# Sample tokens' B rows transposed in threes and masked by VectorE alone; tail steps and weight splits placed later in the first feed-forward steps

## The chip, the cores and the metric

The kernel runs on one core of one Trainium2 chip. The metric is device time in microseconds (us) of one execution. Before the change three runs took 1756.88, 1762.55 and 1763.55 us, a median of 1762.55. The engines are called as the profile calls them: PE (TensorE matmul), PEld (its weight loads), DVE (VectorE), ACT (ScalarE), POOL (GpSimd) and SP (SyncE, which issues the DMAs).

## The reference, cut to what matters

One layer of a hybrid decoder over 1024 prompt tokens and 64 sample tokens (8 sequences of 8), width 1024, all in float32.

```python
h = rmsnorm(x, g_mix_pre) * (1 + scale_m) + shift_m
sc_b, sc_c, sc_x, z, xbc, dt_raw = jnp.split(h @ w_in, idx, axis=-1)
u = sc_c * sc_x
y_sc = sc_b * causal_dwconv(u, sc_buf, sc_conv_w)
xs, Bm, Cm = jnp.split(silu(causal_dwconv(xbc, ssm_buf, ssm_conv_w, ssm_conv_b)), ...)
# SSD, per chunk: y = (C B^T * decay) x dt + C state decay ; state = state * decay + B^T (x dt decay_to_end)
y_ssd, new_state = ssd_scan(xs, dt, A, Bm, Cm, d_skip, ssm_state)
y_ssd = rmsnorm_by_group(y_ssd * silu(z)) * ssm_norm_g
x = x + gate_m * rmsnorm(concat(y_sc, y_ssd) @ w_out, g_mix_post)
h2 = rmsnorm(x, g_ffn_pre) * (1 + scale_f) + shift_f
x = x + gate_f * rmsnorm((silu(h2 @ w_gate) * (h2 @ w_up)) @ w_down, g_ffn_post)
```

Each of the 8 sample sequences has a state of its own in every head, so its new state needs the B rows of that sequence's 8 tokens alone: B masked by sequence.

## The kernel before, in words

Every product is made of float32 parts that are split in two: a value v is rounded to `hi` (by ACT) and `lo = v - hi` (by DVE), and a product is the sum of hi·hi, hi·lo and lo·hi, so three matmuls. The helpers are `split_w` (L308 to L310) and `part` (L1023 to L1025): one ACT cast, one DVE subtraction. A weight tile must be loaded and split before PE can use it.

The stages, in order of time: input norm and first projections (to about 60 us); the SSD scan in four head groups, g = 0 to 3, with the projections of the next group laid between its steps (to about 460 us); gates and the short-convolution group (to about 800 us); output projection (to about 985 us); feed-forward, 11 steps of 256 hidden columns (to about 1470 us), its down projection and the last norm.

An order is set in two ways. Outside helper functions, the program is recorded as Python runs, and a scheduler then places the instructions of each engine; `tc.issue_after(x)` ties what follows behind x. The generators of two pieces of work are advanced in turn (`merge`, `between`), so that PE has one's matmuls while the other waits. Each engine, and SP's queue of DMAs, then runs its own list strictly in that order: an instruction that waits holds all behind it.

**The end of an SSD group.** `ssd` (from L688) runs four pairs of chunks. `part_b` (L737) multiplies chunk results and carries the state S: DVE scales S by the decay (L760) and adds the new part (L763); PE's L754 needs S. In the last of the four pairs, `sample_a` (L773) and `sample_b` (L811) were recorded ahead of `part_b`. `sample_a` transposes x and B of the 64 sample tokens, copies (ACT L799) and subtracts (DVE L800) the two parts of B into `XB`, and copies the last decay of each sequence to `dsm` (DVE L805). `sample_b` builds `BS`, the masked B rows, in six instructions of 32 partitions x 512 (L820): four on POOL, two on DVE. The sample states' products (L876) need `BS`.

**The first feed-forward steps.** The token rows are finished in two tails, `mix_tail` (L1321): `tail_a` for token tiles 4 and 5, `tail_b` for 6, 7 and the samples (8). A tail has five steps: (1) first half of the columns transposed by PE, squared by ACT, scaled by DVE; (2) second half, then the norm and the residual sum; (3) the second norm's factor and an ACT scaling of the rows (L1337); (4) and (5) transposes back (L1345) and ACT's scale and shift (L1347), with the samples' own part (L1353 to L1357, DVE and POOL) in (5). Steps are hung behind PE's blocks of `plain_step` (L1486). One `plain_step(j, q, ...)` makes the 256 hidden columns j for token half q: a gate unit and an up unit, each of four blocks of 24 matmuls, and then `inner_out` (L1503), which makes four pieces of the result and stores each: ACT cast, DVE subtraction, DMA to DRAM (`put`, L1508). All pieces of half 0 go through one buffer, `st0`, so each ACT cast of a piece waits until the DMA of the piece before has read that buffer. `plain_w` loads and splits the weights of a unit; the scheduler was free to place these splits.

Around the change this order holds: step (0,0) with gate and up, step (1,0), then half 1's first step (0,1).

Of the kernel before, what the change touches and what calls it, by code (L numbers as in the profile page):

```python
# [16 lines left out]
P = 128  # L17
# [3 lines left out]
NS = 64  # L21
# [12 lines left out]
def hymba_step(ctx, tc, i, o):  # L34
# [42 lines left out]
    def st(shape, dt=F32):  # L77
        return stp.tile(shape, dt, tag="st", name=nm("st"))
# [10 lines left out]
    def const(shape, name, dt=F32):  # L89
        return cp.tile(shape, dt, tag=name, name=name)  # L90

    def bc(ap, axis, n):
        shape = list(ap.shape)
        shape.insert(axis, n)
        return ap.unsqueeze(axis).broadcast_to(shape)
# [58 lines left out]
    for k in range(4, KT):  # L154
# [18 lines left out]
                            pattern=[[-8, 8]], channel_multiplier=1)  # L173
    nc.gpsimd.affine_select(out=blk, in_=blk, compare_op=ALU.is_ge, fill=0.0, base=7,
                            pattern=[[8, 8]], channel_multiplier=-1)
    blk4 = const([NS, 4], "blk4")
    nc.vector.tensor_tensor(blk4, blk[:, 0:4], blk[:, 4:8], op=add)
    i2 = const([32, 16], "i2")
    nc.vector.tensor_tensor(i2, ident[:32, 0:16], ident[:32, 16:32], op=add)
    selc = const([64, 16], "selc")  # L180
# [382 lines left out]
    r = 0  # L563
# [123 lines left out]
    def ssd(g, x0, x1, Bf, Cf):  # L687
# [86 lines left out]
        def sample_a():  # L774
            tpx, tpb = pz(), pz()
            for p in range(2):
                nc.tensor.transpose(tpx[:NS, p * P:(p + 1) * P], xc[p][:, col:], ident)
            nc.tensor.transpose(tpb[:NS, 0:P], Bf[:, col:], ident)
            mm(tpb[:NS, P:P + NS], Bf[:, col:], Cf[:, col:], start=True, stop=True)
            ac = pz()  # L780
            for r in range(4):
                mm(ac[:, r * NS:(r + 1) * NS], sel(4 * g + r), acT[:, col:], start=True, stop=True)
            xd = st([NS, 2, 4, 64])
            for e, factor in enumerate((dt, edend)):
                nc.vector.tensor_tensor(xd[:, e], tpx[:NS, :256].rearrange("p (r q) -> p r q", r=4),
                                        bc(factor[:NS, 8, hs], 2, 64), op=mult)
            EC = st([P, 3, 4, NS])
            acv = ac[:, :256].rearrange("p (r l) -> p r l", r=4)
            E, Cx = EC[:NS, 0], EC[:, 1]
            nc.scalar.activation(Cx, acv, AF.Exp)  # L790
            nc.vector.tensor_tensor(E, acv[:NS], bc(acum[:NS, 8, hs], 2, NS), op=sub)
            nc.vector.tensor_scalar(E, E, 0.0, None, op0=mn)
            nc.scalar.activation(E, E, AF.Exp)
            CBm = EC[:NS, 2, 0, :]
            nc.vector.tensor_tensor(CBm, tpb[:NS, P:P + NS], utsf, op=mult)

            XB = gzp.tile([96, 768], F32R, tag="gz", name=nm("XB"))
            Bp = XB[:NS, 512:768].rearrange("k (j n) -> k j n", j=2)
            nc.scalar.copy(Bp[:, 0, :], tpb[:NS, 0:P])  # L799
            nc.vector.tensor_tensor(Bp[:, 1, :], tpb[:NS, 0:P], Bp[:, 0, :], op=sub)  # L800
            nc.vector.tensor_tensor(E, E, bc(CBm, 1, 4), op=mult)
            dsm = sp.tile([P, 2, 8], F32, tag="dsm", name=nm("dsm"))
            for p in range(2):
                for h in range(2):
                    nc.vector.tensor_copy(dsm[64 * h:64 * h + 64, p, :],  # L805
                                          bt(Cx[64 * h:64 * h + 64, 2 * p + h, :])[:, :, 7])
            nc.vector.tensor_tensor(Cx, Cx, bc(Cf[:, col:], 1, 4), op=mult)
            return xd, E, Cx, XB, Bp, dsm

        def sample_b(xd, XB, Bp):  # L810
            XS = XB[:, 0:512].rearrange("k (q m) -> k q m", q=2)  # L811
            BS = fm(F32R)[:96, :1024].rearrange("k (q n) -> k q n", q=2)
            for q in range(2):
                own, other = slice(32 * q, 32 * q + 32), slice(32 - 32 * q, 64 - 32 * q)
                v = xd[own, 1].rearrange("k r q -> k (r q)")
                nc.scalar.copy(XS[own, q, :], v)
                nc.scalar.copy(XS[64:96, q, :], v)
                nc.vector.tensor_tensor(XS[other, q, :], v, XS[own, q, :], op=sub)
                for part, at in ((0, own), (0, other), (1, slice(64, 96))):
                    (nc.vector if part else nc.gpsimd).tensor_tensor(  # L820
                        BS[at, q, :].rearrange("k (b n) -> k b n", b=4), bc(Bp[own, part, :], 1, 4),
                        bc(blk4[own], 2, P), op=mult)
            return XS, BS

        def sample_states(p):
# [14 lines left out]
        for j in range(4):  # L840
            if j < 3:
                a2 = part_a(j + 1)
            else:
                a2 = sample_a()
                XS, BS = sample_b(a2[0], *a2[3:5])
            yield
            part_b(j, *a, *m)
            yield
            if j < 3:
                a = a2  # L850
                m = part_m(j + 1, *a)
                yield
# [559 lines left out]
    def plain_x(xp, q):  # L1412
# [10 lines left out]
        X_of[q][3] = new_x(xp, 3, q, b22)  # L1423
        yield

    def behind(gen):

        while True:
            queued = {x.engine: x for x in nc.cur_bb.bb.instructions}
            with ExitStack() as es:  # L1430
                for e in (nc.vector, nc.scalar):
                    es.enter_context(tc.issue_after(queued[e.engine]))
                if next(gen, gen) is gen:
                    return
            yield

    def sums_x(xp, q):
# [17 lines left out]
    def plain_unit(W, q, put, between={}):  # L1455

        X = X_of[q]

        def block(ps, i, h):
            acc3(ps, QS[q][1], [(W[i, j][0][k], W[i, j][1][k], x[0][k], x[1][k])  # L1460
                                for j, x in enumerate((X[(1, 0)[h]], X[(2, 3)[h]])) for k in range(4)])

        for n, (i, h) in enumerate(((0, 0), (0, 1), (1, 0), (1, 1))):
            ps = (pm, pz)[q]()
            in_order(block, ps, i, h)
            put(i, h, ps[:, :QS[q][1]])
            for gen in between.get(n, ()):
                in_order(next, gen, None)
# [9 lines left out]
    def gate_unit(j, qs, W, between={}):  # L1478
# [3 lines left out]
        for q in qs:  # L1482
            v = G_[j, q].rearrange("p m h c -> p (m h c)")
            nc.scalar.activation(v, v, AF.Silu)

    def plain_step(j, q, between):  # L1486

        sg, f = blocks(in_turn(sg_from[q]), q, "sg"), blocks(in_turn(f_from[q]), q, "f")
        plain_unit(plain_w(w_gate, 256 * j), q, lambda i, h, ps: nc.scalar.activation(sg[:, i, h], ps, AF.Silu),
                   between[0])  # L1490
        plain_unit(plain_w(w_up, 256 * j), q,
                   lambda i, h, ps: nc.vector.tensor_tensor(f[:, i, h], sg[:, i, h], ps, op=mult), between[1])
        inner_out(j, q, f, nc.vector)

# [53 lines left out]
    run(px)  # L1548
    out_proj(2, terms[2], {7: [tail_a]}, lambda mp: w_last, (3,))
    tail_b = mix_tail([6, 7, 8], x_tl, row_tl, G2)  # L1550
    plain_step(0, 0, ({0: [tail_b], 1: [tail_b], 2: [tail_a, tail_a], 3: [tail_a]}, {3: [tail_b, tail_b]}))
    raw_from = [btp] * 4
    w_from = [slots[1]] * 4 + [slots[0]] * 4
    g0 = sums_x([xc0], 0)
    s0 = behind(g0)
    plain_step(1, 0, ({0: [tail_b]}, {1: [s0], 2: [s0], 3: [s0]}))
    run(tail_a, tail_b)
    tailp.close()
    xc1 = [pool(left, "xc1a", 1)]
# [177 lines left out]
```

## Time and profile before

| what | value |
|---|---|
| median of 3 runs | 1762.55 us |
| the profiled execution | 1764.2 us, its span 1762.5 us |
| PE busy | 1693.1 us, 96% of the span |
| PE weight loads | 1605.9 us |
| DVE, ACT, POOL busy | 1173.0, 773.5, 231.8 us |
| mean granted TensorE clock | 0.985 |
| HBM traffic | 146 GB/s over the span |

PE is busy nearly everywhere, so what can be won or lost is PE's idle time and the time in which its clock is granted at half. A busy PE is the union of its matmuls' modelled spans, so the share hardly says how fast they run; the clock column of a stage does. A wait row reads: engine, tile and line that waited, what it waited for, total us, times, longest.

### The profile page before, as it was taken

The page shows a single profiled execution, that of the slowest core. Times are in us where ns is not written, and L with a number is a line of the kernel's source. Part 1 is how long each engine was busy: PE and PEld are TensorE (multiplying, and loading weights), DVE is VectorE, ACT ScalarE, POOL GpSimd, SP SyncE. Part 2 cuts the span into 40 slices and gives each one's busy share as a digit, 9 for nine tenths or more (in the row PEclk, how much of TensorE's full clock was granted, in tenths as well). Part 3 has the DMA queues.
Part 4 walks back from the last instruction along what each step waited for, and adds up shares of the span by engine and source line. Part 5 has one row for each costly group of instructions (what it writes and reads, how often), then busy time and mean ns, then how long its engine had stood idle before and what let it go on. Part 6 is the DMA issues. An engine that isn't in the chain of part 4 may idle for free. (4 is left out here: it accounts for less than half of the span.)

```text
span 1762.5 us, 31586 instructions
## 1 busy us (share of the span) xinstructions
PE 1693.1 (96%) x12624; PEld 1605.9 (91%) x12624; DVE 1173.0 (67%) x2263; ACT 773.5 (44%) x1595; POOL 231.8 (13%) x333
## 2 busy tenths in 40 slices
PE   5999999999999999999999899999999999899997
PEld 4898888899999999998989899999999998799987
DVE  5578787867797676651137769666665575678845
ACT  3447454557344333322227765444444454322303
POOL 2111020201000000000000000122222201322303
PEclk9999999999899999999999999999999999999999
DMA  9301345442312422268275634344444439755243
GB/s 314 74 19 43 104 130 182 129 126 76 125 49 99 150 78 66 86 215 283 71 243 188 201 114 149 105 149 147 148 151 143 147 134 347 288 223 229 100 153 120
DMA packets 160634, 259.74 MB, mean 147 GB/s; under 512 B 10561, under 2 KB 124401, under 8 KB 158182
## 3 DMA queue, kind: packets, MB, share of 16 engines
q1 hardware_dynamic: 160486, 257.71, 42.8%
q8 instruction: 99, 1.62, 0.4%
q14 instruction: 49, 0.40, 0.1%
HBM read 186.30 MB, written 71.38 MB: 146 GB/s over the span
## 5 line engine op out<-in xcount | busy, mean ns | idle before, releaser
L310 DVE TENSOR_TENSOR wl<-raw,wh 128x512 fp32r<-128x512 f32 (+1 forms) x87 | 61.4, 730 | 101.2 <-ACT wh L309 97.5
L333 PE MATMUL pm<-h,wh 128*128 128x384 f32 (+1 forms) x342 | 115.2, 337 | 0.0
L332 PE MATMUL pm<-h,wh 128*128 128x384 f32 (+1 forms) x342 | 115.1, 337 | 0.0
L334 PE MATMUL pm<-h,wl 128*128 128x384 f32 (+1 forms) x342 | 114.4, 336 | 0.0
L334 PE MATMUL pm<-hb,wl 128*128 128x512 f32 (+2 forms) x320 | 107.4, 337 | 1.9 <-DVE wl L310 1.9
L333 PE MATMUL pm<-hb,wh 128*128 128x512 f32 (+2 forms) x320 | 107.3, 337 | 0.0
L332 PE MATMUL pm<-hb,wh 128*128 128x512 f32 (+2 forms) x320 | 105.4, 337 | 1.3 <-ACT wh L309 1.3
L309 ACT CAST wh<-raw 128x512 fp32r<-128x512 f32 (+1 forms) x89 | 56.5, 664 | 109.8 <-PE pm L333 66.7
L1025 DVE TENSOR_TENSOR fs<-f,fs 128x512 fp32r<-128x512 f32 (+1 forms) x80 | 55.4, 706 | 25.9 <-ACT fs L1024 25.4
L1024 ACT CAST fs<-f 128x512 fp32r<-128x512 f32 (+1 forms) x80 | 46.7, 598 | 49.9 <-DMA f_d<-fs 31.6
L334 PEld LDWEIGHTS pm<-hb,wl 128*128 128x128 f32 x320 | 60.7, 190 | 7.4 <-DVE wl L310 2.1
L332 PEld LDWEIGHTS pm<-h,wh 128*128 128x128 f32 x342 | 65.5, 192 | 1.9 <-issue 1.0
L1080 DVE TENSOR_TENSOR facc<-facc,pz 128x288 f32<-128x288 f32 x124 | 55.9, 451 | 16.7 <-PE pz L1065 16.4
L332 PEld LDWEIGHTS pm<-hb,wh 128*128 128x128 f32 x320 | 60.5, 190 | 7.0 <-ACT wh L309 1.6
L333 PEld LDWEIGHTS pm<-h,wh 128*128 128x128 f32 x342 | 65.4, 191 | 1.1 <-issue 0.3
L334 PEld LDWEIGHTS pm<-h,wl 128*128 128x128 f32 x342 | 65.4, 191 | 0.9 <-issue 0.9
L333 PEld LDWEIGHTS pm<-hb,wh 128*128 128x128 f32 x320 | 60.7, 190 | 5.2
L1080 DVE TENSOR_TENSOR facc<-facc,pm 128x256 f32<-128x256 f32 x124 | 51.5, 415 | 6.5 <-PE pm L1065 6.3
L332 PE MATMUL pm<-bt,wh 128*128 128x384 f32 (+1 forms) x146 | 51.4, 352 | 0.0
L1042 POOL TENSOR_TENSOR raw<-raw 128x512 f32<-128x512 f32 x16 | 22.5, 1404 | 206.7 <-DVE raw L1040 206.7
L334 PE MATMUL pm<-bt,wl 128*128 128x384 f32 (+1 forms) x146 | 48.5, 332 | 0.3 <-DVE wl L310 0.2
L333 PE MATMUL pm<-bt,wh 128*128 128x384 f32 (+1 forms) x146 | 48.1, 330 | 0.0
(7508 smaller groups left out, 6405.7 us busy)
## 6 DMA issues: line engine op xcount, KB each, us to landing
raw<-in_w_in SPq DMA_DIRECT2D x48, 512.0 KB
fc<-f_d SPq DMA_DIRECT2D x9, 2016.0 KB
f_d<-fs SPq DMA_DIRECT2D x31, 576.0 KB
wa<-in_w_ada SPq DMA_DIRECT2D x32, 512.0 KB
raw<-in_w_out SPq DMA_DIRECT2D x32, 512.0 KB
fc<-f_d SPq DMA_DIRECT2D x9, 1792.0 KB
f_d<-fs SPq DMA_DIRECT2D x31, 512.0 KB
raw<-in_w_gate SPq DMA_DIRECT2D x28, 512.0 KB
```

The source lines that it names most:

```text
L309: (nc.gpsimd.tensor_copy if hi_eng else nc.scalar.copy)(wh, raw)
L310: (eng or nc.vector).tensor_tensor(wl, raw, wh, op=sub)
L332: mm(ps[:, :n], wh, xh, start=(first and j == 0), stop=False)
L333: mm(ps[:, :n], wh, xl, start=False, stop=False)
L334: mm(ps[:, :n], wl, xh, start=False, stop=(last and j == end))
L1024: nc.scalar.copy(hi, v)
L1025: (eng or nc.vector).tensor_tensor(lo, v, hi, op=sub)
L1042: eng.tensor_tensor(a21, a11, a21, op=sub)
L1080: nc.vector.tensor_tensor(out(q, i, h), out(q, i, h), ps, op=add)
```

## The change

1. `sample_a`: ACT first copies B of the sample tokens three times side by side (into an unused part of the tile `EC`), and two transposes of 96 rows (one for each half of the tokens) set B's rows on partitions 0 to 31, 32 to 63 and 64 to 95. The CB product moves to other columns of the same bank. One ACT copy of 96 x 256 and one DVE subtraction of 32 x 256 make the parts.
2. `sample_b`: the six masking instructions become two on DVE, of 64 x 1024 and of 32 x 1024. POOL has none. The constant `blk4` grows to 96 rows.
3. `sample_b` is recorded behind `part_b` of the last pair.
4. First feed-forward steps: `tail_b`'s second step one block later; `tail_a`'s steps 3, 4, 5 at gate block 3, up blocks 0 and 1 (before: two at gate block 2, one at 3); `tail_b`'s step 4 at the next step's gate block 0, step 5 at its block 1.
5. `step_w`: in every step with j > 0 that is made by `plain_step`, that is step (1,0), the loads and splits of both weight units are recorded through `last_in_line`, which ties their first instruction on DVE and ACT behind everything recorded so far on these engines.

```diff
-    blk4 = const([NS, 4], "blk4")
-    nc.vector.tensor_tensor(blk4, blk[:, 0:4], blk[:, 4:8], op=add)
+    blk4 = const([96, 4], "blk4")
+    nc.vector.tensor_tensor(blk4[:NS], blk[:, 0:4], blk[:, 4:8], op=add)
+    nc.vector.tensor_copy(blk4[NS:], blk4[:32])
...
-            nc.tensor.transpose(tpb[:NS, 0:P], Bf[:, col:], ident)
-            mm(tpb[:NS, P:P + NS], Bf[:, col:], Cf[:, col:], start=True, stop=True)
+            EC = st([P, 3, 4, NS])
+            B3 = EC[:, 2, 1:4].rearrange("p a (h n) -> p (a h) n", h=2).rearrange("p (q r) n -> p q r n", q=2)
+            nc.scalar.copy(B3, bc(Bf[:, col:].rearrange("p (q n) -> p q n", q=2), 2, 3))
+            for q in range(2):
+                nc.tensor.transpose(tpb[:96, q * P:(q + 1) * P], B3[:, q].rearrange("p r n -> p (r n)"), ident)
+            mm(tpb[:NS, 256:256 + NS], Bf[:, col:], Cf[:, col:], start=True, stop=True)
...
-            Bp = XB[:NS, 512:768].rearrange("k (j n) -> k j n", j=2)
-            nc.scalar.copy(Bp[:, 0, :], tpb[:NS, 0:P])
-            nc.vector.tensor_tensor(Bp[:, 1, :], tpb[:NS, 0:P], Bp[:, 0, :], op=sub)
+            Bp = XB[:, 512:768]
+            nc.scalar.copy(Bp, tpb[:96, 0:256])
+            nc.vector.tensor_tensor(Bp[NS:], tpb[NS:96, 0:256], Bp[NS:], op=sub)
...
-                for part, at in ((0, own), (0, other), (1, slice(64, 96))):
-                    (nc.vector if part else nc.gpsimd).tensor_tensor(
-                        BS[at, q, :].rearrange("k (b n) -> k b n", b=4), bc(Bp[own, part, :], 1, 4),
-                        bc(blk4[own], 2, P), op=mult)
+            for at in (slice(0, NS), slice(NS, 96)):
+                nc.vector.tensor_tensor(BS[at].rearrange("k q (b n) -> k q b n", b=4),
+                                        bc(Bp[at].rearrange("k (q n) -> k q n", q=2), 2, 4),
+                                        bc(bc(blk4[at], 1, 2), 3, P), op=mult)
...
                 a2 = sample_a()
-                XS, BS = sample_b(a2[0], *a2[3:5])
             yield
             part_b(j, *a, *m)
+            if j == 3:
+                XS, BS = sample_b(a2[0], *a2[3:5])
             yield
...
+    def last_in_line(f, *a):
+
+        queued = {x.engine: x for x in nc.cur_bb.bb.instructions}
+        with ExitStack() as es:
+            for e in (nc.vector, nc.scalar):
+                es.enter_context(tc.issue_after(queued[e.engine]))
+            return f(*a)
+
     def behind(gen):
...
+        while last_in_line(next, gen, gen) is not gen:
             yield
...
+    def step_w(w, j):
+        return last_in_line(plain_w, w, 256 * j) if j else plain_w(w, 256 * j)
+
...
-        plain_unit(plain_w(w_gate, 256 * j), q, lambda i, h, ps: nc.scalar.activation(sg[:, i, h], ps, AF.Silu),
+        plain_unit(step_w(w_gate, j), q, lambda i, h, ps: nc.scalar.activation(sg[:, i, h], ps, AF.Silu),
                    between[0])
-        plain_unit(plain_w(w_up, 256 * j), q,
+        plain_unit(step_w(w_up, j), q,
                    lambda i, h, ps: nc.vector.tensor_tensor(f[:, i, h], sg[:, i, h], ps, op=mult), between[1])
...
-    plain_step(0, 0, ({0: [tail_b], 1: [tail_b], 2: [tail_a, tail_a], 3: [tail_a]}, {3: [tail_b, tail_b]}))
+    plain_step(0, 0, ({0: [tail_b], 2: [tail_b], 3: [tail_a]}, {0: [tail_a], 1: [tail_a], 3: [tail_b]}))
...
-    plain_step(1, 0, ({0: [tail_b]}, {1: [s0], 2: [s0], 3: [s0]}))
+    plain_step(1, 0, ({0: [tail_b], 1: [tail_b]}, {1: [s0], 2: [s0], 3: [s0]}))
```

Lines below the first hunk have other numbers after the change (L1024 becomes L1031, L310 becomes L312, and so on). Numbers behind a tile's name tell buffers apart; those of the two kernels don't match.

VectorE at the end of group 0, before (`wl` is the low part of the next group's first weight tile, `st`, `XB`, `dsm` and `fm` are the sample tokens' tiles, `S` the carried state):

```order
L310 TENSOR_TENSOR wl_1978<-raw_1975,wh_1977 128x1024
L791 TENSOR_TENSOR st_1811<-pz_1803,acum 64x256
L800 TENSOR_TENSOR XB_1817<-pz_1798,XB_1817 64x128
L792 TENSOR_SCALAR st_1811<-st_1811 64x256
L805 COPY dsm_1821<-st_1811 64x8 x4
L818 TENSOR_TENSOR XB_1817<-st_1808,XB_1817 32x256
L801 TENSOR_TENSOR st_1811<-st_1811 64x256
L807 TENSOR_TENSOR st_1811<-st_1811,fm_1311 128x256
L820 TENSOR_TENSOR fm_1827<-XB_1817,blk_259 32x512
L818 TENSOR_TENSOR XB_1817<-st_1808,XB_1817 32x256
L820 TENSOR_TENSOR fm_1827<-XB_1817,blk_259 32x512
L763 TENSOR_TENSOR S_1882<-S_1882,pz_1866 128x256
```

The weight split stands ahead of all the sample work, and the addition to S behind all of it.

The same engine and place after the change; L826 is the masking that was L820, L765 the addition to S, L425 to L429 a convolution of the next group, L312 the weight split:

```order
L813 TENSOR_TENSOR st_1802<-st_1802,fm_1312 128x256
L762 TENSOR_TENSOR S_1872<-S_1736,ecd 128x256
L824 TENSOR_TENSOR XB_1820<-st_1812,XB_1820 32x256
L765 TENSOR_TENSOR S_1872<-S_1872,pz_1856 128x256
L824 TENSOR_TENSOR XB_1820<-st_1812,XB_1820 32x256
L762 TENSOR_TENSOR S_1879<-S_1872,ecd 128x256
L826 TENSOR_TENSOR fm_1884<-XB_1820,blk_259 64x1024
L765 TENSOR_TENSOR S_1879<-S_1879,pz_1856 128x256
```

Both additions to S now stand ahead of the second masking instruction. Further on in the same list, the end of the convolution and what follows it:

```order
L428 SCALAR_TENSOR_TENSOR fm_1939<-ext_1771,vT,fm_1939 128x1024
L429 SCALAR_TENSOR_TENSOR fm_1939<-ext_1771,vT,fm_1939 128x64
L868 COPY st_1952<-pz_1949 128x256
L312 TENSOR_TENSOR wl_1977<-raw_1974,wh_1976 128x1024
L884 TENSOR_TENSOR s_237_1893<-s_237_1893,dsm_1824 128x1024
L884 TENSOR_TENSOR s_251_2007<-s_251_2007,dsm_1824 128x1024
```

The split of `wl_1977`, the same tile as `wl_1978` before, has moved from ahead of the sample work to behind the masks, the convolution and the copy L868. On PE the first matmuls that need it (L336) have moved behind the other parts of the next group's first blocks and the first two sample states' products.

ScalarE where step (0,0) passes into step (1,0), before (`fs` are the stored pieces of step (0,0), `wp` 1195 to 1198 the gate weights of step (1,0), `sg` a gate block's result, L1337 the rows' scaling, L1347 the samples' and tokens' scale and shift):

```order
L1337 ACTIVATE x_10152<-x_10152,sm_10469 64x1024
L1024 CAST wp__1195_10527<-raw_10523 128x512
L1024 CAST wp__1196_10530<-raw_10525 128x512
L1024 CAST wp__1197_10533<-raw_10523 128x512
L1024 CAST wp__1198_10536<-raw_10525 128x512
L1347 ACTIVATE acc_8215<-pz_10485,modT,A_f 128x256
L1347 ACTIVATE acc_8215<-pz_10489,modT,A_f 128x256
L1347 ACTIVATE acc_8215<-pz_10493,modT,A_f 128x256
L1347 ACTIVATE acc_8215<-pz_10497,modT,A_f 128x256
L1024 CAST fs_10501<-f_10105 128x512
L1489 ACTIVATE sg_10521<-pm_10539 128x256
```

The weights' casts stand ahead of every stored piece; the other three pieces are cast later still. The same after the change, where the gate weights are `wp` 1191 to 1194:

```order
L1344 ACTIVATE x_10145<-x_10145,sm_10462 64x1024
L1031 CAST fs_10478<-f_10098 128x512
L1031 CAST fs_10482<-f_10098 128x256
L1031 CAST fs_10488<-f_10098 128x512
L1031 CAST fs_10494<-f_10098 128x512
L1031 CAST wp__1191_10504<-raw_10500 128x512
L1031 CAST wp__1192_10507<-raw_10502 128x512
L1031 CAST wp__1193_10510<-raw_10500 128x512
L1031 CAST wp__1194_10513<-raw_10502 128x512
L1500 ACTIVATE sg_10498<-pm_10516 128x256
```

All four pieces now stand ahead of the first weight, and the four casts L1354 that stood between have gone behind the gate block. VectorE's subtractions of these tiles follow in the same order.

ScalarE during step (0,0)'s gate blocks, before, where the up weights of step (1,0), `wp` 1210 and 1211, were first cast (L1229 and L355 belong to the tails):

```order
L1489 ACTIVATE sg_10104<-pm_10122 128x256
L1024 CAST wp__1210_10688<-raw_10684 128x512
L355 ACTIVATE tl_9978,ssn<-x_9974 128x1024
L1024 CAST wp__1211_10691<-raw_10686 128x512
L355 ACTIVATE tl_9979,ssn<-x_9976 128x1024
L1229 ACTIVATE tl_10154,ss_10157<-pz_10159 128x512
L1229 ACTIVATE tl_10155,ss_10157<-pz_10166 128x512
L1489 ACTIVATE sg_10104<-pm_10180 128x256
```

The casts are spread between the tails' work, a whole unit ahead of their use.

ScalarE where step (1,0) passes from gate to up, after (`wp` 1210 to 1213 are its up weights, 1233 and 1234 a part of the next step's, `x__1227` the samples' operand of half 1):

```order
L1500 ACTIVATE sg_10498<-pm_10625 128x256
L1031 CAST x__1227_10841<-acc_8208 128x1152
L1031 CAST wp__1233_10853<-raw_10848 128x512
L1031 CAST wp__1234_10856<-raw_10846 128x512
L1500 ACTIVATE sg_10498<-pm_10651 128x256
L1031 CAST wp__1210_10681<-raw_10677 128x512
L1031 CAST wp__1211_10684<-raw_10679 128x512
L1031 CAST wp__1212_10687<-raw_10677 128x512
L1031 CAST wp__1213_10690<-raw_10679 128x512
```

The same up weights now stand behind the last gate block's evacuation of step (1,0), behind `x__1227` and behind two weights of the next step.

More of the change, by code (lines that the diff above doesn't have):

```diff
@@ L786, in sample_a @@
                                         bc(factor[:NS, 8, hs], 2, 64), op=mult)
-            EC = st([P, 3, 4, NS])
             acv = ac[:, :256].rearrange("p (r l) -> p r l", r=4)
@@ L794, in sample_a @@
             CBm = EC[:NS, 2, 0, :]
-            nc.vector.tensor_tensor(CBm, tpb[:NS, P:P + NS], utsf, op=mult)
+            nc.vector.tensor_tensor(CBm, tpb[:NS, 256:256 + NS], utsf, op=mult)
             XB = gzp.tile([96, 768], F32R, tag="gz", name=nm("XB"))
-            Bp = XB[:NS, 512:768].rearrange("k (j n) -> k j n", j=2)
-            nc.scalar.copy(Bp[:, 0, :], tpb[:NS, 0:P])
-            nc.vector.tensor_tensor(Bp[:, 1, :], tpb[:NS, 0:P], Bp[:, 0, :], op=sub)
+            Bp = XB[:, 512:768]
+            nc.scalar.copy(Bp, tpb[:96, 0:256])
+            nc.vector.tensor_tensor(Bp[NS:], tpb[NS:96, 0:256], Bp[NS:], op=sub)
             nc.vector.tensor_tensor(E, E, bc(CBm, 1, 4), op=mult)
@@ L1424, in plain_x @@
         yield
-    def behind(gen):
[L1428 to L1434, printed above, removed]
+    def last_in_line(f, *a):
[4 more added lines that the diff above has]
+            return f(*a)
+    def behind(gen):
+        while last_in_line(next, gen, gen) is not gen:
             yield
```

## The prediction

> **What bounds the kernel now.** I read the page first, then PE's waits, then the stretches around the two longest. In the page's row of engines each entry is the busy time, its share of the span and the instructions:
>
> ```profile
> PE 1693.1 (96%) x12624; PEld 1605.9 (91%) x12624; DVE 1173.0 (67%) x2263; ACT 773.5 (44%) x1595; POOL 231.8 (13%) x333
> ```
>
> PE sets the time. What the change can touch is PE's idle time and its half-clock time. The waits of PE in its places are (total, times, longest):
>
> ```profile
> PE pz L754 <- DVE S L763: 4.5, 2, 2.8
> PE pz L1228 <- DVE tl L1230: 3.1, 1, 3.1
> PE pz L1345 <- ACT x L1337: 3.1, 2, 2.7
> ```
>
> The first is the end of SSD groups 0 and 3; the other two stand in the first feed-forward steps. The windows show the steps, a clean comparison behind them, and the clock at the end of groups 0 and 3 (after the engines: PEclk, DMA share, GB/s):
>
> ```profile
> core 0: us, PE busy (x) PEld busy (x) DVE busy (x) ACT busy (x) POOL busy (x), PEclk, DMA share, GB/s
> ...
> 175.28:182.00 6.72, 3.94 (x19) 3.69 (x19) 6.65 (x14) 1.07 (x4) 0.74 (x2) 0.75 0.00 1
> ...
> 441.36:444.77 3.41, 1.70 (x16) 1.26 (x15) 3.38 (x8) 1.35 (x3) 0.00 (x0) 1.00 0.00 0
> 444.77:448.18 3.41, 3.41 (x16) 3.37 (x15) 2.84 (x7) 1.84 (x4) 0.00 (x0) 0.50 0.00 0
> ...
> 455.01:461.84 6.83, 6.83 (x47) 5.80 (x46) 3.19 (x9) 0.10 (x1) 0.00 (x0) 0.50 0.25 77
> ...
> 986.26:1011.61 25.35, 19.04 (x139) 17.17 (x138) 20.61 (x67) 17.41 (x42) 0.13 (x1) 0.93 0.59 202
> 1011.61:1023.36 11.75, 11.75 (x100) 11.75 (x100) 3.54 (x8) 6.70 (x11) 0.00 (x0) 1.00 0.01 1
> ```
>
> Half clock comes in pieces of 3.41 us and follows a gap: PE was busy 1.70 of 3.41, and the next 3.41 ran at 0.50. Such a piece costs PE half of itself, 1.7 us. Group 0's stretch holds one too (0.75 over 6.72 us).
>
> **The tail's transposes (part 4): a gain.** PE's rows in the first stretch:
>
> ```profile
> 989.21 1.47 PE L1228 MATMUL pz<-ident,acc 128*128 128x128 f32 x12
> ...
> 997.09 1.65 PE L1228 MATMUL pz<-ident,acc 128*128 128x128 f32 x8 [3.09 <-DVE tl L1230]
> ...
> 1005.45 0.65 PE L1345 MATMUL pz<-ident,x 128*128 128x128 f32 x4 [2.75 <-ACT x L1337]
> 1006.49 0.66 PE L1345 MATMUL pz<-ident,x 128*128 128x128 f32 x4 [0.39 <-ACT x L1337]
> ...
> 1010.06 1.79 PE L1345 MATMUL pz<-ident,x 128*128 128x128 f32 x8
> ```
>
> Four blocks take 11.75 us where nothing disturbs them. The first stretch holds four blocks and 40 transposes; at 1.47 / 12 = 0.12 us these are 4.8, so 25.35 - 16.55 = 8.8 us are lost: 6.2 of idle time, 1.7 of clock (0.93 is 1 - 0.07, and 0.07 x 25.35 = 1.8 of half clock's loss), the rest bank waits. Each awaited step now stands one block, 2.9 us, later or more, so the three waits go. What is late next is the bank: 8 transposes took 1.79 instead of 0.96, and two such groups leave 2 x 0.8 = 1.6. The gain is **7.2** (5 to 8).
>
> **Weights behind the stores (part 5, gate): a loss.** Step (1,0)'s first gate weight now stands on ACT and DVE behind all four stored pieces of step (0,0), which share one buffer. Rows of the chain:
>
> ```profile
> 1025.73 0.63 ACT L1024 CAST fs<-f 128x512 fp32r<-128x512 f32 x1
> ...
> 1037.81 0.68 DVE L1025 TENSOR_TENSOR fs<-f,fs 128x512 fp32r<-128x512 f32 x1
> 1041.26 0.62 ACT L1024 CAST fs<-f 128x512 fp32r<-128x512 f32 x1 [2.70 <-DMA f_d<-fs]
> ...
> 1058.10 0.42 DVE L1025 TENSOR_TENSOR fs<-f,fs 128x256 fp32r<-128x256 f32 x1
> 1061.14 0.62 ACT L1024 CAST fs<-f 128x512 fp32r<-128x512 f32 x1 [0.16 <-DVE f L1521]
> ```
>
> A store blocks the next cast from the end of the subtraction, 1037.81 + 0.68 = 1038.49, to 1041.26: 2.77 us. For the half-sized piece the bound is 1061.14 - 1058.52 = 2.6. In before the weights stood ahead of this, so the 2.77 hid behind PE's block. Now, from the end of PE's last up block: the product 0.42 (by its size, as the 128x256 row); piece 1, 0.63 + 0.68; store 2.77; piece 2, 0.42 + 0.42; store 2.6; piece 3, 0.63 + 0.68; store 2.77; piece 4's cast 0.62, then DVE's subtraction 0.68 and the weight's own, of the same size, 0.68. That is 14.0 us. PE has two matmuls that need the rounded part alone, and nothing else: the tail steps are hung behind the gate block. So **+13.8** idle (13 to 14.5; lower if piece 2's store is faster). PE then restarts at half clock; one piece is 1.7 (0 to 3.4). Together **+15.5**.
>
> **Weights behind the evacuation (part 5, up): a loss.** The up weights now stand behind the samples' operand `x__1227`, whose steps read:
>
> ```profile
> 1028.09 0.71 PE L1353 MATMUL pz<-ident,x 64*128 64x64 f32 x8
> 1029.14 4.31 POOL L1357 TENSOR_TENSOR acc<-acc,modT 128x64 f32<-128x64 f32 x8 [26.92 <-DVE acc L1356]
> 1033.49 1.16 ACT L1024 CAST x__1227_10848<-acc 128x1152 fp32r<-128x1152 f32 x1 [0.15 <-POOL acc L1357]
> ...
> 1035.27 1.35 DVE L1025 TENSOR_TENSOR x__1227_10848<-acc,x__1227_10848 128x1152 fp32r<-128x1152 f32 x1
> ```
>
> From PE's L1353 (28.80) to the cast's end (34.65) are 5.85 us; then 1.35 and two weight splits of 0.68 on DVE make 8.6. PE covers it with gate blocks 2 and 3 and two matmuls, 5.9 + 0.2. The wait is **+2.5** (0 to 4), and with one chance in two of a half-clock piece +0.8: **+3.3**.
>
> Behind both, DVE is full where half 1 begins, and PE waited for it there once:
>
> ```profile
> 1049.15:1080.75 31.60, 30.86 (x230) 30.45 (x229) 30.89 (x43) 18.51 (x30) 0.00 (x0) 1.00 0.31 111
> 1080.76 0.40 PE L1065 MATMUL pz<-x__1227_10848,w__1267_11175 128*128 128x288 f32 x1 [0.74 <-DVE w__1267_11175 L1025]
> ```
>
> The splits moved later join this queue, 30.89 busy of 31.60: **+1.0** (0 to 3). The tail in all: -7.2 + 15.5 + 3.3 + 1.0 = **+12.6**.
>
> **The samples' part (1 to 3): a small gain in group 3, a trade in group 0.** Group 0's rows:
>
> ```profile
> 168.79 1.21 DVE L310 TENSOR_TENSOR wl<-raw,wh 128x1024 fp32r<-128x1024 f32 x1
> 168.53 1.28 ACT L790 ACT_TABLE_LOAD   x1
> 170.24 0.42 DVE L791 TENSOR_TENSOR st<-pz,acum 64x256 f32<-64x256 f32 x1 [0.24 <-ACT st L790]
> 170.44 4.65 POOL L820 TENSOR_TENSOR fm<-XB,blk 32x512 fp32r<-32x512 f32 x4 [7.85 <-ACT XB L799]
> 171.54 2.20 DVE L805 COPY dsm<-st 64x8 f32<-64x8 f32 x4
> 178.06 0.72 PE L754 MATMUL pz<-st,S 128*64 128x128 f32 x8 [2.78 <-DVE S L763]
> 179.40 0.47 DVE L767 SCALAR_TENSOR_TENSOR fm<-fm,dcol,pz 128x256 f32<-128x256 f32 x1
> 180.51 0.81 DVE L423 TENSOR_SCALAR fm<-ext,vT 128x1024 f32<-128x1024 f32 x1
> ...
> 185.44 0.28 DVE L427 SCALAR_TENSOR_TENSOR fm<-ext,vT,fm 128x64 f32<-128x64 f32 x1
> 185.84 1.03 PE L832 MATMUL pz<-ident,s 128*128 128x128 f32 x8
> ...
> 189.27 0.62 PE L876 MATMUL pz<-fm,XB 96*128 96x512 f32 x2
> 189.82 0.64 PE L870 MATMUL pz<-st,st 128*64 128x8 f32 x16
> ```
>
> While POOL masked, a `dsm` copy took DVE 0.55 us. All sixteen such copies of the run (least, median and most in ns):
>
> ```profile
> L805 DVE COPY dsm<-st x16: 154/542/922, 171.5 to 437.2; 64x8 f32<-64x8 f32 x16
> ```
>
> I take the least, 0.15, for all of them after the change. A mask over 1024 columns should need 1.21, as the split at 168.79 does.
>
> The sample work on DVE starts at about 168.9 rather than 170.24, since ACT's table load now stands ahead of the copy that held it, and the split is gone from here. Eight instructions of at most 0.42 and four copies of 0.15 bring S to 172.8. PE comes there with 18 products of 0.15 still ahead of its old stop at 175.28, so at 172.5: a wait of 0.3, and the 2.78 goes. But the split now follows masks, convolution and a copy. On DVE: three of 0.42 and a mask to S's second addition, 175.3; two updates of 0.47 and a mask, 177.4; the convolution (180.51 to 185.72) 5.2, 182.6; the copy 0.42, 183.0; the split, **184.2**. PE meanwhile has moved forward what needs no `wl`: half of the S products 0.36, two transposes of S 0.25 (by the eight in 1.03), four sample products 0.2 and sixteen 0.64, eight transposes 1.03, six weight products 1.1 (384 columns, by 11.75 / 96 for 256), two state products 0.62. These 4.2 us put it at 175.28 + 4.2 + 0.3 = 179.8. The new wait is 4.4 and the net 4.4 + 0.3 - 2.8 = **+1.9** (-2 to +4; the low end is a wait of 2.2 with no half-clock piece, 1.7, in its wake).
>
> In group 3 no such split moves. The 1.71 and the piece of 1.7 behind it go, and of the 6.83 us at 0.50 later (3.4 lost) I take 1.0 as following from the same gap: **-4.4** (-1.7 to -6.8). Groups 1 and 2 show no wait: 0. An extra transpose a group, 4 x 0.12, is +0.5. The sum here is 1.9 - 4.4 + 0.5 = **-2.0**. The work taken from POOL hid behind PE wherever DVE did not stand still for it, and costs nothing.
>
> In all 12.6 - 2.0 = +10.6. The profiled execution has a span of 1762.5, and with what lies around it 1764.2; the median is 1762.55, which I take as the base: **1773.2 us**.
>
> **A rule on the clock.** Here 1.71 us of idle time was enough for half clock. The Trainium skill's "TensorE: Matmul & The Clock Gate", section "HAM oscillation — how this bites in real kernels", warns of idle gaps above about 3.4 us. By that rule the 0.8 of the up wait would fall away and the time would be 1772.4. This trace speaks against the threshold with its 1.71.
>
> **Rivals.** *Half clock ends throughout groups 0 and 3, so the kernel is not slower beyond what can be told:* 6.8 instead of 4.4 in group 3 and 1.7 in group 0 give 4.1 less, 1769.1. It decides from 1.8 below my sum. For it: a gap stands ahead of the piece at 444.77; against: at 455 PE was not idle, and group 0 keeps a gap by my own sum. *The trade in group 0 is dearer:* if ACT's table load still comes when it did, `wl` is 1.4 later; with a second half-clock piece behind the long stall, 1.7, and DVE's queue at 3 instead of 1, 1778.3. *The change does not do what it says:* if DVE's copies stay at 0.55 without POOL's masks, S is late as before and group 3's 4.4 is not won: 1777.6. *The stores do not serialise three times:* if only one waits, 2.77 + 2.6 less, 1767.8.
>
> **How the numbers follow.** About 0.5%, 8.8 us, is what a measurement of this kernel can tell from no change, so 1771.4 divides "slower" from "same". My forecast has 0.52 (its own range 1769 to 1777, two thirds above the line); the clock rival 0.18, the dear trade 0.15, the unchanged masks 0.05, the stores 0.06. The 0.04 left is for faster: the gate stall would have to be absent (1757.7) and the clock rival true besides (1753.6, below the other line at 1753.7). Slower: 0.34 + 0.15 + 0.05 + 0.02 = 0.56; same: 0.18 + 0.16 + 0.06 = 0.40. The range 1764 to 1780 takes in all but the ends.
>
> **What would show it.** Right: a PE gap of 13 to 14 us ahead of step (1,0)'s first gate block, released by DVE or ACT on a `wp` tile, with casts of `fs` waiting for DMAs in it, and half clock behind it; a gap of about 2.5 ahead of its up unit; no L1230 wait near 994; in group 0 a wait for `wl` instead of S; `dsm` copies near 0.15. Wrong: PE running through that boundary, or stores that end within a block.

## The result, and the profile after

The changed kernel takes 1775.3 us, the median of 6 runs (1769.9 to 1779.13), beside 1762.72 (1756.88 to 1763.55, 6 runs) before. The ratio is 1.0073, 95% interval 1.0051 to 1.0095: it is slower by 12.9 us (9 to 17). The prediction was 1773.2, 10.6 more. Its profiled execution has a span of 1775.4 us.

PE's waits after the change, in the places that the prediction speaks of and in two that it doesn't (`wp__653` and `h`):

```profile
PE pm L334 <- ACT wp__1191_10504 L1031: 12.8, 1, 12.8
...
PE pm L336 <- DVE wp__653_5031 L1032: 2.6, 1, 2.6
...
PE pz L883 <- DVE st L868: 2.1, 1, 2.1
...
PE pm L334 <- ACT wp__1210_10681 L1031: 1.8, 1, 1.8
PE pz L1352 <- ACT x L1344: 1.6, 2, 1.2
...
PE pm L1070 <- ACT h L1031: 1.2, 1, 1.2
```

The waits for S (4.5) and for `tl` (3.1) are gone. In their place stands one gap of 12.8 us, ahead of step (1,0)'s first gate block, as forecast. ACT's list in it shows the chain (start, duration, and in brackets how long ACT stood idle ahead of the cast and what ended it):

```profile
1020.75 0.62 ACT L1031 CAST fs<-f 128x512 fp32r<-128x512 f32 x1 [1.79 <-DVE f L1503]
1024.80 0.40 ACT L1031 CAST fs<-f 128x256 fp32r<-128x256 f32 x1 [3.43 <-DMA f_d<-fs]
1027.78 0.62 ACT L1031 CAST fs<-f 128x512 fp32r<-128x512 f32 x1 [2.58 <-DMA f_d<-fs]
1031.83 0.62 ACT L1031 CAST fs<-f 128x512 fp32r<-128x512 f32 x1 [3.43 <-DMA f_d<-fs]
1032.35 0.61 ACT L1031 CAST wp__1191_10504<-raw 128x512 fp32r<-128x512 f32 x1
```

Three casts wait for the DMA of the piece before, and only then comes the weight. VectorE's and PE's rows of the same chain:

```profile
1021.40 0.69 DVE L1032 TENSOR_TENSOR fs<-f,fs 128x512 fp32r<-128x512 f32 x1 [0.68 <-ACT fs L1031]
1025.23 0.43 DVE L1032 TENSOR_TENSOR fs<-f,fs 128x256 fp32r<-128x256 f32 x1 [3.14 <-ACT fs L1031]
...
1028.43 0.69 DVE L1032 TENSOR_TENSOR fs<-f,fs 128x512 fp32r<-128x512 f32 x1 [0.94 <-ACT fs L1031]
...
1033.02 0.58 PE L334 MATMUL pm<-x__1114_9935,wp__1191_10504 128*128 128x256 f32 x1 [12.76 <-ACT wp__1191_10504 L1031]
```

From the end of a subtraction to the next cast are 1024.80 - 1022.09 = 2.71, 1027.78 - 1025.66 = 2.12 and 1031.83 - 1029.12 = 2.71 us (forecast 2.77, 2.6, 2.77). The gap, the stretch of half clock behind it, and what follows (PEclk is the first number behind the engines):

```profile
core 0: us, PE busy (x) PEld busy (x) DVE busy (x) ACT busy (x) POOL busy (x), PEclk, DMA share, GB/s
1020.26:1033.02 12.76, 0.00 (x1) 0.00 (x1) 4.47 (x9) 2.83 (x6) 0.00 (x0) 0.65 0.25 103
1033.02:1037.63 4.61, 4.59 (x20) 4.30 (x21) 2.56 (x5) 1.51 (x3) 0.00 (x0) 0.50 0.55 180
1037.63:1049.73 12.10, 12.04 (x102) 11.53 (x101) 6.09 (x13) 9.72 (x17) 4.32 (x8) 1.00 0.18 63
```

PE then ran 4.6 us at half clock, which costs 2.3, and at full clock from there to the up unit's wait. In group 0 the wait is now this (rows of DVE and PE, in order of time):

```profile
182.57 0.41 DVE L868 COPY st<-pz 128x256 f32<-128x256 f32 x1
182.91 1.21 DVE L312 TENSOR_TENSOR wl<-raw,wh 128x1024 fp32r<-128x1024 f32 x1
...
183.04 0.73 PE L883 MATMUL pz<-fm,XB 96*128 96x512 f32 x2 [2.12 <-DVE st L868]
...
184.17 0.59 PE L336 MATMUL pm<-bt,wl 128*128 128x384 f32 x1 [0.40 <-DVE wl L312]
```

And the `dsm` copies, without POOL's masks beside them:

```profile
L811 DVE COPY dsm<-st x16: 153/166/170, 169.5 to 439.6; 64x8 f32<-64x8 f32 x16
```

To compare places in two traces I subtract the times of the same instruction. PE's wait ahead of group 0 that ends at 130.00 us (before at 129.15) comes 0.85 later; that is ahead of all that was changed in the work. The end of the tail's region (PE's wait for `w__1267` ended at 1095.42, before at 1080.76) comes 14.66 later, its start (the wait for `wl` ended at 948.50, before at 945.14) 3.36 later. So 11.3 us of the 12.9 lie in the first feed-forward steps, 2.5 between 130 and 945 us, and behind 1095 the changed kernel regains 1.8.

### The profile page after: what moved, and what is told of

Read it like the earlier page. It is cut to its first block, busy times and chain, and to the rows that moved or that the text cites. A ratio compares the mean times of both kernels' runs of the same rounds, so it can differ in the third digit from the quotient of the medians.

```text
span 1775.4 us, 31579 instructions
## 1 busy us (share of the span) xinstructions
PE 1694.9 (95%) x12628; PEld 1608.4 (91%) x12628; DVE 1167.5 (66%) x2264; ACT 778.1 (44%) x1601; POOL 213.8 (12%) x317
## 4 chain that ended last, share of the span: by engine, by line
PE 79%; DVE 9%; DMA 5%; ACT 3%; issue 2%; POOL 1%; SPq 1%; DVEq 0%; POOLq 0%; ACTq 0%
PE pm L334 10%; PE pm L336 10%; PE pm L335 9%; PE pz L1072 7%; PE pz L1070 7%; PE pz L1071 7%; PE pm L1070 6%; PE pm L1072 6%; PE pm L1071 6%; DMA h<-in_w_ada 1%; DMA raw<-in_w_in 1%; PE pm L209 1%; PE pz L751 1%; PE pz L745 1%; PE pz L756 1%
## 5 line engine op out<-in xcount | busy, mean ns | idle before, releaser
L312 DVE TENSOR_TENSOR wl<-raw,wh 128x512 fp32r<-128x512 f32 (+1 forms) x87 | 61.3, 729 | 100.8 <-ACT wh L311 97.4
L336 PE MATMUL pm<-h,wl 128*128 128x384 f32 (+1 forms) x342 | 115.0, 337 | 0.0
L336 PE MATMUL pm<-hb,wl 128*128 128x512 f32 (+2 forms) x320 | 107.4, 337 | 1.9 <-DVE wl L312 1.9
L1031 ACT CAST fs<-f 128x512 fp32r<-128x512 f32 (+1 forms) x80 | 46.6, 597 | 59.3 <-DMA f_d<-fs 37.5
L336 PEld LDWEIGHTS pm<-hb,wl 128*128 128x128 f32 x320 | 60.8, 190 | 7.4 <-DVE wl L312 2.1
L336 PEld LDWEIGHTS pm<-h,wl 128*128 128x128 f32 x342 | 66.1, 193 | 1.3 <-issue 1.0
L334 PE MATMUL pm<-bt,wh 128*128 128x384 f32 (+2 forms) x146 | 52.0, 356 | 0.0
L336 PE MATMUL pm<-bt,wl 128*128 128x384 f32 (+1 forms) x146 | 48.8, 334 | 0.6 <-DVE wl L312 0.6
L335 PE MATMUL pm<-bt,wh 128*128 128x384 f32 (+2 forms) x146 | 48.1, 330 | 0.0
```

The costliest lines, as they stand in the source:

```text
L312: (eng or nc.vector).tensor_tensor(wl, raw, wh, op=sub)
L334: mm(ps[:, :n], wh, xh, start=(first and j == 0), stop=False)
L335: mm(ps[:, :n], wh, xl, start=False, stop=False)
L336: mm(ps[:, :n], wl, xh, start=False, stop=(last and j == end))
L1031: nc.scalar.copy(hi, v)
```

## The experiments

Ten kernels, each timed in five rounds against the kernel before on the same chip. Differences in us are the ratio less one, times 1762. The theory is the prediction's: the weights behind the stores (part 5) make the loss, part 4 wins, and the samples' part (1 to 3) about breaks even. The rival that the first trace raised is that the samples' part loses, behind group 3, where the waits for `wp__653` and `h` are new.

**Part 5 undone.**

```diff
     def step_w(w, j):
-        return last_in_line(plain_w, w, 256 * j) if j else plain_w(w, 256 * j)
+        return plain_w(w, 256 * j)
```

> Parts 1 to 4 with part 5 undone. If the 14 us stall in front of step (1,0) and the wait at its up unit come from the weights tied behind the stores (part 5), both are gone from the profile and the kernel takes 1763 - 7.2 (tail) - 2.0 (samples) = 1753 to 1757 us. If the stall comes from the new places of the tail steps (part 4), it stays and the time stays near 1775.

Measured 1758.34 us, ratio 0.998 (0.9971 to 0.9989), -3.5 us. The gap of 12.8 and the up unit's wait are gone from the trace. So part 5 costs 1.0073 - 0.998 = 0.0093, 16 us. The time is 1 us over the upper end of what was expected: the other parts win less. Its trace also shows a new wait of 1.65 us for ACT's `sg`, near 1071 us where half 1 begins; the kernel before and the one with part 4 alone have none there.

**Parts 1 to 3 alone** (the lines of parts 4 and 5 set back).

> Parts 1 to 3 alone. By the prediction's sum 2.0 us less than before, 1760.7; by the rival that the half-clock pieces of groups 0 and 3 go, 6.1 less, 1756.6; by the dear trade in group 0, 0 to 2 us more, 1763 to 1765. The profile of the full change shows a wait of 2.6 for a weight behind group 3, which was 0.9: if the samples' part makes it, it is seen here too and the time is 1764 or more.

1763.05 us, 1.0004 (0.9994 to 1.0014). The waits behind group 3 are here too, so the samples' part makes them. PE's rows there, of this kernel: the norm's products L291, where VectorE's stretch begins, and the three waits:

```profile
461.61 1.50 PE L291 MATMUL pz<-ident,sm 128*128 128x128 f32 x12
...
483.08 0.46 PE L336 MATMUL pm<-bt,wp__653_5031 128*128 128x384 f32 x1 [2.59 <-DVE wp__653_5031 L1032]
...
522.79 0.39 PE L1070 MATMUL pm<-h,w__683_5285 128*128 128x272 f32 x1 [1.21 <-ACT h L1031]
...
523.95 0.39 PE L1071 MATMUL pm<-h,w__683_5285 128*128 128x272 f32 x1 [0.77 <-DVE h L1032]
```

The same instructions of the kernel before:

```profile
464.96 1.60 PE L289 MATMUL pz<-ident,sm 128*128 128x128 f32 x12
...
486.09 0.44 PE L334 MATMUL pm<-bt,wp__653_5038 128*128 128x384 f32 x1 [0.91 <-DVE wp__653_5038 L1025]
...
524.55 0.39 PE L1064 MATMUL pm<-h,w__683_5292 128*128 128x272 f32 x1 [0.52 <-DVE h L1025]
```

At L291 this kernel is 3.35 us ahead, at `wp__653` 3.0, at the last 0.6. It wins three microseconds in the SSD stage and gives them back in the next 60. VectorE shows why; the windows are from L291 to the first of these waits and from there to the second, before:

```profile
464.96:486.03 21.07, 20.22 (x128) 19.68 (x127) 19.72 (x29) 9.53 (x17) 0.00 (x0) 1.00 0.69 231
486.03:523.65 37.62, 37.13 (x248) 36.70 (x248) 37.27 (x60) 16.92 (x33) 0.00 (x0) 1.00 0.19 57
```

and with parts 1 to 3:

```profile
461.61:483.02 21.41, 18.88 (x121) 18.34 (x120) 20.21 (x30) 9.60 (x17) 0.00 (x0) 1.00 0.67 228
483.02:522.80 39.78, 38.52 (x248) 38.29 (x248) 37.32 (x60) 16.77 (x33) 0.00 (x0) 0.96 0.18 54
```

DVE is busy 37.3 of 37.6 us before, so it has nothing to spare there, and PE's waits in this stretch end with VectorE's work or with a cast. In the first window PE now has 18.9 us of work instead of 20.2, and waits for about the same 20 us of DVE. In the second DVE has the same 37.3 us of work, and what makes it 2.2 us longer is PE's waits and two half-clock pieces that follow them, 3.4 us lost:

```profile
483.38:486.79 3.41, 3.41 (x12) 3.41 (x11) 3.41 (x7) 1.04 (x2) 0.00 (x0) 0.50 0.07 6
524.34:527.75 3.41, 3.41 (x18) 3.41 (x17) 1.61 (x4) 0.53 (x2) 0.00 (x0) 0.50 0.00 0
```

**Part 4 alone.**

```diff
-    plain_step(0, 0, ({0: [tail_b], 1: [tail_b], 2: [tail_a, tail_a], 3: [tail_a]}, {3: [tail_b, tail_b]}))
+    plain_step(0, 0, ({0: [tail_b], 2: [tail_b], 3: [tail_a]}, {0: [tail_a], 1: [tail_a], 3: [tail_b]}))
...
-    plain_step(1, 0, ({0: [tail_b]}, {1: [s0], 2: [s0], 3: [s0]}))
+    plain_step(1, 0, ({0: [tail_b], 1: [tail_b]}, {1: [s0], 2: [s0], 3: [s0]}))
```

> Part 4 alone. Prediction: the waits at 994 and 1003 and the half-clock piece between them go, 7.2 us less than before, 1755.5 (5 to 8). Rival: the waits only move to other steps, less than 2 us gained, 1761 or more.

1755.71 us, 0.9967 (0.9955 to 0.998), -5.8 us: the fastest complete kernel of the study, ahead of both. The wait for `tl` is gone; those for ACT's scaling are smaller, not gone, and in this trace a half-clock piece still follows them (from 1004.55):

```profile
1002.49 0.66 PE L1345 MATMUL pz<-ident,x 128*128 128x128 f32 x4 [1.65 <-ACT x L1337]
1003.53 0.66 PE L1345 MATMUL pz<-ident,x 128*128 128x128 f32 x4 [0.38 <-ACT x L1337]
```

**Part 5 alone** (`last_in_line` and `step_w` added to the kernel before, the tail steps in their old places).

> Part 5 alone, with the tail steps in their old places. Prediction's chain of three stores: a gap of 12.5 to 14 us ahead of step (1,0)'s gate unit, half clock behind it, and little at its up unit since the samples' rows are done earlier: 15 to 17 us more than before, 1778 to 1780. Rival, that the stall needs the tail steps' new places: less than 5 us more, under 1768.

1781.02 us, 1.0109 (1.0095 to 1.0123), +19.2 us, 1 us over the upper end expected. The stall needs nothing of part 4:

```profile
1038.33 0.58 PE L332 MATMUL pm<-x__1114_9942,wp__1195_10527 128*128 128x256 f32 x1 [13.47 <-ACT wp__1195_10527 L1024]
...
1055.46 0.38 PE L332 MATMUL pm<-x__1114_9942,wp__1210_10688 128*128 128x256 f32 x1 [0.98 <-ACT wp__1210_10688 L1024]
```

**Only the up unit's weights tied** (the gate unit calls `plain_w` again).

```diff
-        plain_unit(step_w(w_gate, j), q, lambda i, h, ps: nc.scalar.activation(sg[:, i, h], ps, AF.Silu),
+        plain_unit(plain_w(w_gate, 256 * j), q, lambda i, h, ps: nc.scalar.activation(sg[:, i, h], ps, AF.Silu),
```

> The full change with only the up unit's weights of step (1,0) tied in line, the gate unit's free. If the gate tie carries the loss, the 12.8 us gap is gone and what stays above 1758.3 (parts 1 to 4 alone) is the up unit's wait, 1.8 as in the full change: 1760 us, with half clock behind it 1762. If the up tie carries a large part, 1766 or more.

1761.58 us, 0.9993 (0.9981 to 1.0005): 2.3 us over the kernel without part 5. The gate's stall is gone. The up unit's wait is 3.30 instead of 1.79, and 6.83 us of half clock come with it (from 1032.22), where none came with 1.79. The wait is longer because POOL's steps for the samples (L1364), which stand ahead of `x__1227`, took 6.15 us here and 4.32 in the full change. So the gate tie carries 14 of part 5's 16 us.

**A second buffer for the stored pieces** of steps (0,0) and (1,0).

```diff
     tlp = pool(tailp, "tlp", 9)
+    st0b = pool(tailp, "st0b", 1)
...
+    st_from.append(st0b)
     plain_step(0, 0, ...)
+    st_from.remove(st0b)
```

> The full change, with a second buffer for the stored pieces of steps (0,0) and (1,0). The order then has three pieces ahead of the gate weights and one wait for a store instead of three. If the stores through one buffer make the gap: 0.42 + 1.31 + 1.3 to 2.8 + 1.31 + 0.68 = 5 to 6.5 us instead of 12.8, and the time 1768 to 1769. Rival, that the gap is the weights' own loads or the evacuations: it stays above 11 and the time stays at 1775.

1766.43 us, 1.0023 (1.0013 to 1.0034): 8.8 us less than the full change. The gap is 8.74 us shorter. No cast ahead of the weight waits for a DMA any more, and the three store waits of the full change were 7.5 us. The rest is the order, which the second buffer changed too: the 128x256 piece is cast ahead of the last product (1017.68), and the fourth piece behind the weights (1024.55):

```profile
1023.13 0.58 PE L334 MATMUL pm<-x__1114_9938,wp__1191_10507 128*128 128x256 f32 x1 [4.02 <-ACT wp__1191_10507 L1031]
```

The stores through one buffer are thereby shown to make the greater part of the stall; how much the new order alone is worth was not tried apart.

**VectorE relieved behind group 3**, with parts 1 to 3 and with the kernel before. Both leave out eight subtractions of the short convolution's block sums, so they compute other sums than the reference there.

```diff
-            nc.vector.tensor_tensor(b11, b12, b11, op=sub)
             part(X_t[5][k][:, 0], X_t[5][k][:, 1], b11)
             yield
-            nc.vector.tensor_tensor(b22, b22, b11, op=sub)
             part(X_t[6][k][:, 0], X_t[6][k][:, 1], b22)
```

> Parts 1 to 3 with eight of VectorE's subtractions of 0.72 us behind group 3 left out (the short convolution's sums of blocks are then not those of the reference). If VectorE, full from the norm on, gives back there what the samples' part won before, the waits of 2.6, 1.2 and 0.8 us shrink to under 1 in all, the two half-clock pieces behind them go, and the time falls from 1763.0 to 1755 to 1757. If the pieces come with something else, 1761 or more.

> The kernel before with the same eight subtractions left out. It waits there only 0.9, 0.4 and 0.5 and has no half-clock piece: 1.8 less at most, 1760.6 to 1762.4. The distance to the run with parts 1 to 3 is then what these parts win ahead of VectorE's full stretch: 3 us if the theory holds, none if it falls.

With parts 1 to 3: 1755.72 us, 0.996 (0.9944 to 0.9975), -7.0, which is 7.7 less than the same parts with the subtractions. The waits of 2.6, 1.2 and 0.8 have become these, and neither half-clock piece is there:

```profile
PE pm L1070 <- ACT h L1031: 0.4, 1, 0.4
PE pm L1071 <- DVE h L1032: 0.4, 1, 0.4
...
PE pm L336 <- DVE wp__653_5027 L1032: 0.4, 1, 0.4
```

The kernel before: 1758.99 us, 0.9976 (0.9966 to 0.9987), -4.2, where at most 1.8 was expected; its three waits are gone, and the rest is not explained. In its trace, 6.5 us shorter than that of the kernel before, only 1.2 lie between PE's waits for S (441.28) and for `w__726` (565.34), which is within what was expected. 2.1 lie ahead and 3.2 behind, where nothing was left out; at 945 us 1.5 of it is a half-clock piece that did not come. How much of the 4.2 is of that kind the times don't tell. The distance of the two, 2.8 us in favour of the samples' part, is what the theory said, but the intervals are as wide as it; the traces carry this point, not the times.

**Parts 1, 2 and 4**, `sample_b` recorded ahead of `part_b` again.

```diff
                 a2 = sample_a()
+                XS, BS = sample_b(a2[0], *a2[3:5])
             yield
             part_b(j, *a, *m)
-            if j == 3:
-                XS, BS = sample_b(a2[0], *a2[3:5])
```

> Parts 1, 2 and 4, the samples' masks ahead of the last carried state as before. The weight split of group 0 then stands where it stood, and S is late by less. If what the samples' part wins is given back on VectorE behind group 3 whatever its size, the time is that of part 4 alone or 1 to 2 us above it, 1755.5 to 1758. If the loss in parts 1 to 4 came from part 3 (the split behind the convolution in group 0, a wait of 2.1), the time is 3 us below part 4 alone, 1752 to 1753.

1760.66 us, 0.9984 (0.9972 to 0.9996), -2.8: neither case. Group 0 has no wait over 0.3 now, so more is won there, and the wait behind group 3 is larger, with two half-clock pieces in a row behind it:

```profile
484.38 0.69 PE L336 MATMUL pm<-bt,wp__653_5031 128*128 128x384 f32 x1 [3.65 <-DVE wp__653_5031 L1031]
```

That what is won comes back as a wait there holds; that it comes back at no greater price doesn't. But the time holds another loss, away from group 3. Where half 1 begins, PE waits for `sg` as with parts 1 to 4, and here half clock follows (1076.94, 6.83 us):

```profile
PE pz L1069 <- ACT sg L1084: 1.8, 1, 1.8
```

**Parts 1 to 4 with the block sums later**, so that the split of `wp__653` stands earlier on VectorE.

```diff
-    gate_late(2, ..., {n: [sums] for n in range(6)})
+    gate_late(2, ..., {n: [sums] for n in range(3)})
```

> Parts 1 to 4, with three of the six steps of the short convolution's sums in gate group 2 put later, so that the weight's split stands 2 us earlier on VectorE. If a gap of 2.6 brings a half-clock piece and a smaller one does not, the first wait falls to about 1, its piece goes, and the time is 1.7 to 3 us under that of parts 1 to 4, 1755.5 to 1756.6. If VectorE only waits elsewhere (a larger gap near 521), it stays at 1758.

1758.79 us, 0.9978 (0.9964 to 0.9993): as parts 1 to 4 were. The wait at 480 is gone, and others stand further on, with a half-clock piece behind (510.55). At 563 a wait for `w__726` has grown from 0.9 to 1.3, and two more pieces follow it (565.16):

```profile
508.41 0.39 PE L1070 MATMUL pm<-x__634_4858,w__680_5275 128*128 128x272 f32 x1 [0.99 <-ACT w__680_5275 L1031]
...
509.94 0.39 PE L1072 MATMUL pm<-x__634_4858,w__680_5275 128*128 128x272 f32 x1 [1.02 <-DVE w__680_5275 L1032]
```

The rival held: here another order on the full engine moved the waits and did not shorten the kernel.

## Why the prediction was right, point by point

- **Weights behind the stores, +15.5: right.** The gap is 12.76 and its half clock costs 2.3, 15.1 in all. Of the 13.8 for the gap, two terms were too large: the smaller store (2.12, not 2.6), and piece 4's subtraction and the weight's own (1.36), which PE doesn't wait for, since its first product needs the cast alone (cast at 1032.35, product at 1033.02). The weight's cast, about 0.6, was left out of the sum. The half clock is larger than one piece's 1.7: it began in the idle time, and the piece in which PE restarted (1030.81 to 1034.22) held only 1.2 us of work, so that the next was at half as well.
- **Weights behind the evacuation, +3.3: right in kind.** The wait is 1.79, and no half clock followed it.
- **VectorE where half 1 begins, +1.0: nothing came of it.** PE waited 0.75 there, before 0.74.
- **The tail's transposes, -7.2: larger than the median shows.** Alone they are worth -5.8 (interval -7.9 to -3.5, which still holds -7.2). The step "the three waits go" failed: ACT's scaling still holds PE for 1.2 to 1.7 and 0.4 us in every run with part 4. Against that, of the 1.6 forecast for the bank at most 0.8 came: one group of eight transposes took 1.8 us in five of these seven kernels and 1.0 in the two others, where a half-clock piece ran just ahead, and the later groups took 1.0 in the full change and with part 4 alone. That these two errors largely offset each other is luck. With all these errors the tail in all is +11.3 in the trace, where 12.6 was forecast.
- **Group 0, +1.9: the wait was found, its releaser not.** The split of `wl` ended at 184.12, forecast 184.2. But PE came later, and most of its wait, 2.12, is L883's, for the copy L868 that stands behind the same convolution; 0.40 is for `wl`. That is 0.3 less idle time than before.
- **Group 3, -4.4: about right in the group itself.** The wait of 1.71 went. Half-clock pieces between 444 and 465 us number 3, 4, 3 and 4 in the four runs without the samples' part, and 3, 1, 1, 1, 1, 3 and 1 in the seven with parts 1 to 3, so 1.9 fewer on average, 3.2 us; with parts 1 and 2 but not 3 there are 3. The clock rival had that much truth.
- **The samples' part in all, -2.0: too low, +0.7 (-1.1 to 2.5).** The gain of 2.0 is outside the interval; whether the part costs or wins a little is open. The step that failed is the sum itself: it took what PE wins in the SSD stage as won to the end. Behind group 3 VectorE is full, and there it becomes waits and, in every run with parts 1 to 3 that keeps all of VectorE's work, half-clock pieces.
- **The sum, +10.6 beside +12.9**, was nearer than its terms by luck: a tail 1.3 too dear offset half of a samples' part 2.7 too cheap. The 0.9 that is left is well inside the interval. What carried the forecast is the gate stall, and that was found by its mechanism.
- **The rule on the clock.** The sum by the rule was right not to charge the up wait, but the rule does not give the reason: 1.71 us brought half clock and 1.79 did not. The last section says on what such cases depend; for these two it doesn't settle it.

## What to carry to other kernels

Before you tie work to the end of an engine's list, read what waits there: here four stored pieces through one buffer, three times 2.1 to 2.7 us of DMA that had been free because nothing stood behind it. Before you count a gain on the bounding engine, look at which engine is full in the next stage: a gain that arrives there turns into a wait, and a wait can cost clock as well. Test the parts of a change apart: one of the five is worth -5.8 us alone, and the whole costs 12.9.

## What the runs showed of the hardware that was not expected

**Half clock is decided in fixed pieces of 3.413 us.** In each trace all half-clock stretches start a whole number of 3.413 us apart (178.529 and 444.768 before: 78.0 pieces). I laid that grid over all twelve traces, from about 24 us after the start to 15 us before the end, and counted, for each piece at full clock, how long PE was busy in it and whether the next was at half:

```
PE busy in the piece (us)   next at half   next at full
under 1.55                            63              0
1.55 to 1.95                          25             25
1.95 to 2.3                            2             34
2.3 to 3.4                             0            494
all of it                             22           5231
```

So in these traces a piece in which PE is busy for less than 1.55 of its 3.41 us always brought half clock, one with 1.55 to 1.95 did in half of the cases, and above that it was rare as long as PE was idle at all. A short gap therefore counts by where the grid cuts it. The clearest case is one wait that all twelve traces have, 1.9 us for `wl` at 945 us of the kernel before: in nine of them its piece held 1.51 or 1.52 us of work, and half clock followed; in three it held 1.60 to 1.74, and none did. The wait of 1.71 in group 3 left 1.70 us of work in its piece, and the up unit's of 1.79 left 1.85; half clock followed the first and not the second, but both lie in the band where either happens. The 22 cases with PE busy throughout all begin between 90 and 95 us or between 444 and 455 us, among many small matmuls; what decides there was not tried. The Trainium skill, "TensorE: Matmul & The Clock Gate", section "Part 1: The HAM clock gate (the "warmup" mystery)", says that the window is 3413 ns and free-running, and these traces agree (3.413 in each). It says that the clock drops after an idle window; here a window idle by half was enough.

**VectorE and POOL hold each other up.** The median of 542 ns for the 64x8 copies before is no copy's time: eight of the sixteen took 154 to 164 ns and eight 919 to 922, all beside POOL's masks. The short ones lie where a mask of 1.06 us just begins (in group 0 a copy and a mask both at 171.54), the long ones begin about 0.15 us into a mask and end 0.03 us behind it (172.63 and 172.60). Without the masks all took 153 to 170. The other way round it is the same: POOL's step L1364 takes 0.3 us, and 1.4 where it begins inside one of VectorE's splits of 1.45 us. Two of the eight steps do so in the full change, 4.32 us in all; with the up unit's weights alone tied three do, and one more takes 0.74 beside a stored piece's split of 0.78, 6.15 in all. The five kernels with part 4 and without the gate weights tied all show 6.15 or 6.16, the seven others 4.31 or 4.32. That the stored pieces among VectorE's splits make this difference was not tried.
